# Layer 0's head norms take raw squares, and key weights are cast ahead of them

## The chip, the cores and the metric

The kernel runs on one core of a Trainium2 chip. The metric is the device time of one execution in microseconds, the median of several runs. A core has a matrix engine (TensorE, PE in the profile; its weight loads are PEld), a vector engine (VectorE, DVE), a scalar engine (ScalarE, ACT), GpSimd (POOL) and SyncE (SP), whose queue issues nearly all transfers. Each engine works through a queue of its own in a fixed order and waits on semaphores for the others.

## The reference

A two-layer encoder on 256 tokens of width 1024 (float32). What matters here is the beginning of a layer:

```python
u = rms_norm(h, g_mix_pre)
(gq, gk, gv, gg, ra_f, ra_b, aq, ak, av, gate_a, gate_b) = jnp.split(u @ w_in, offsets, axis=-1)
...
q = apply_axial_rope(rms_norm(aq.reshape(b, s, ATTN_HEADS, HEAD_DIM), g_q_norm), cos, sin)
k = apply_axial_rope(rms_norm(ak.reshape(b, s, ATTN_KV_HEADS, HEAD_DIM), g_k_norm), cos, sin)
```

Here `rms_norm(x, g)` is `x * rsqrt(mean(x*x) + 1e-6) * g`. There are 8 query heads and 2 key/value heads of 128. `ra_f` and `ra_b` are 16 columns each, the low-rank inputs of the decay of a gated linear attention (GLA). After that come both attentions, gates, an output projection, a feed-forward block and a per-layer embedding.

## The kernel before, in words

**Precision.** Every operand of a product is split into a high part (ScalarE casts it) and a low part (VectorE subtracts the cast from the source); three matmuls make one product. `split` does this for any tile (its lines are 132 and 128 of the profile).

**Weights.** All weights come in an ordered stream of units of about 1 MB. A unit is loaded into one of two raw buffers (`raw`), then cast into `wh` and subtracted into `wl`, each in two pieces (four such pairs of buffers); only after the subtraction is the raw buffer free for the next load. In layer 0, units 0 to 3 are the rows of the weights of the decay ranks and the queries together (1056 columns), units 4 and 5 the two halves of the key/value weights, units 6 and 7 those of the GLA queries. `Stream.fill` puts the splits of further units in the program as earlier ones are done. `ws.pieces` hands out the pieces of units 0 to 2, whose splits the start writes out by hand.

**Tokens.** The 256 tokens are two halves of 128 (`hf` 0 and 1).

**Start of layer 0.** The input norm is not applied to the tokens before the projection. `start` transposes raw blocks of `h` by TensorE into PSUM (`turn`), ScalarE scales by the gain column and casts (`high`), VectorE makes the low part (`rest`); the matmuls begin on these. `rstd` computes meanwhile, on GpSimd, the factor `rs[hf]` of each token: the sum of two mean squares and epsilon, then the power -1/2. It is multiplied in wherever the projection's results are read. A chain `on(engine, ...)` fixes the order of these instructions on each engine by hand. `warm_up` issues matmuls without a result in between.

**Ranks and queries** (`0rq`). For each half, three accumulators of 288, 384 and 384 columns take the product with units 0 to 3. When one is complete, `put_q` reads it: `put_ranks` (first accumulator only) scales the ranks into a zeroed tile with two columns of ones, which TensorE transposes some steps later (L987); `head_ss` squares each head on ScalarE with the sum beside it (L960), scaling by `rs`; `inv_sqrt` turns the sums into factors on GpSimd: add epsilon (L457), power (L458), and for layer 0 times `rs` (L461); `rope` rotates on VectorE (L125 twice, L954 once). The head's factor is used only in the softmax.

**Keys and values** (`0kv`). 48 matmuls of 512 columns with units 4 and 5 into two accumulators, one for each half; `keys` does the norm and rotation. Then come the GLA queries and keys (`0gqk`), the values and so on, with steps of the attention and the GLA put between the matmuls at fixed counts (`tick`).

**What sets the order.** Instructions are written in a program order; a planner places them in the queues before the run, by priority. `tc.high_priority(n)` moves a block ahead by n; `put_q` of layer 0 has `EMPTY_FIRST` = 1600. `tc.issue_after(ins)` puts the instructions of a block behind `ins` in the queue of that engine, without a semaphore. PSUM has eight banks, each an `acc` or `aux` tile.

Of the kernel before, what the change touches and what calls it, by code (L numbers as in the profile page):

```python
# [10 lines left out]
F32 = mybir.dt.float32  # L11
# [3 lines left out]
ALU = mybir.AluOpType  # L15
AX = mybir.AxisListType

P = 128
# [40 lines left out]
def trunk_kernel(ctx: ExitStack, tc: tile.TileContext, a: dict, out: bass.AP):  # L59
# [67 lines left out]
    def vsub(out, in0, in1):  # L127
        nc.vector.tensor_tensor(out=out, in0=in0, in1=in1, op=ALU.subtract)  # L128

    def split(hi, lo, src):  # L130

        nc.scalar.copy(hi, src)  # L132
        vsub(lo, src, hi.bitcast(F32))


    h = cp.tile([P, 2, D], F32, tag="h", name="h")
# [111 lines left out]
    class Stream:  # L248
# [7 lines left out]

        def __init__(self, depth):
            self.depth, self.held, self.room, self.ready, self.open = depth, 0, 0, [], False
            self.loads, self.jobs, self.lend = [], [], False
            pairs = {}  # L260
            for item in plan:
                if callable(item):
                    x = Load(item)
                    self.loads.append(x)
                    self.jobs.append(lambda x=x: self.plain(x))
                else:
                    units, n = item
                    if n == 1:
                        b11, b12, b21, b22 = units
                        x, z = (Load(b, lambda tag=tag: self.lent(tag), tag == "wh") for b, tag in ((b11, "wh"), (b12, "wl")))  # L270
                        y, q = Load(b22, big), Load(b21)
                        pairs[id(units)] = x, y, z, q
                        self.loads += [x, y, z]
                    if n == 5:
                        self.loads.append(q)
                    self.jobs.append(lambda p=pairs[id(units)], n=n: self.step(n, *p))
# [69 lines left out]

        def fill(self):
            while self.open and self.held < self.depth and self.jobs:
                pieces = self.jobs.pop(0)()
                for piece in pieces or ():  # L350
                    split(*piece)
                if pieces:
                    self.load()

        def take(self):
            self.fill()
# [5 lines left out]
            self.fill()  # L362

    ws = Stream(4)


    def gain(v, t, n):
# [83 lines left out]

        return tc.issue_after(last_pow[0].ins) if last_pow[0] is not None else nullcontext()

    def inv_sqrt(t, n, mul, add, by=None):

        with in_turn():
            nc.gpsimd.tensor_scalar(out=t, in0=t, scalar1=mul, scalar2=add, op0=ALU.mult, op1=ALU.add)  # L457
        last_pow[0] = nc.gpsimd.tensor_tensor(out=t, in0=t, in1=neghalf[:, :n], op=ALU.pow)  # L458
        if by is not None:
            with in_turn():  # L460
                last_pow[0] = nc.gpsimd.tensor_scalar(out=t, in0=t, scalar1=by, scalar2=None, op0=ALU.mult)  # L461

    def split_by(hi, lo, src, r):

# [289 lines left out]
    warm_up(WARM[1], True)  # L754
    uT = Split()
    ss = [small(2, "ss") for _ in range(2)]
    rs, ropes_first = [small(1, "rs", 2) for _ in range(2)], []

    up_first = [mid()]
    on("pool", nc.gpsimd.memset, up_first[0][0:81, :], 0.0)  # L760
# [9 lines left out]
    def rstd(hf):  # L770
        on("pool", nc.gpsimd.tensor_scalar,
           out=rs[hf], in0=ss[hf][:, 0:1], scalar1=ss[hf][:, 1:2], scalar2=EPS, op0=ALU.add, op1=ALU.add)
        on("pool", nc.gpsimd.tensor_tensor, out=rs[hf], in0=rs[hf], in1=neghalf[:, 0:1], op=ALU.pow)
        last_pow[0] = line["pool"]

# [37 lines left out]
    def start():  # L813
        cut = lambda piece, c: [t[:, c] for t in piece]
        gains()
        turn(0, 0)
        turn(1, 0)
        turn(0, 1)
        turn(1, 1)
        turn(0, 2, 3)  # L820
        warm_up(WARM[2], True)
        high(0, 0)
        high(1, 0)
        for c in RQ:
            on("act", nc.scalar.copy, *(t[:, slice(*c)] for t in unit_a[::2]))
        rest(0, 0)
        rest(1, 0)
        low(*cut(unit_a, slice(0, 288)))
        high(0, 1)
        high(1, 1)  # L830
        low(*cut(unit_a, slice(288, 1056)))
        on("act", nc.scalar.copy, unit_b[0], unit_b[2])
        rest(0, 1)
        rest(1, 1)
        high(0, 2, 3)
        low(*unit_b)
        rest(0, 2, 3)
        ws.load()
        unit_c, unit_d = ws.pieces()
        yield 2  # L840
        turn(1, 2, 3)
        high(1, 2, 3)
        rest(1, 2, 3)
        yield 4
        split_here(*unit_c)
        split_here(*unit_d)
        ws.load()
        for hf in range(2):
            square(hf, 0)
        yield 2  # L850
        turn(0, 4, 5, 6, 7)
        for hf in range(2):
            square_here(hf, 1)
            rstd(hf)
        ropes_first.extend(rope_tables(0))
        high(0, 4, 5, 6, 7)
        rest(0, 4, 5, 6, 7)
        yield 1
        turn(1, 4, 5, 6, 7)
        high(1, 4, 5, 6, 7)  # L860
        rest(1, 4, 5, 6, 7)
        for piece in ws.pieces():
            split_here(*piece)
        ws.load()
        ws.open = True
        ws.fill()
# [59 lines left out]
    for l in range(DEPTH):  # L926

        part[0] = f"{l}rq"
        rows = [None, None] if l else rs
        after_start = tc.issue_after(line["dma"].ins) if l == 0 else nullcontext()  # L930
        if l == 0:
            ropes = ropes_first
# [20 lines left out]
            )  # L953
            nc.vector.tensor_tensor(out=hv(dst), in0=hv(dst), in1=hv(t2), op=ALU.add)  # L954

        def head_ss(src, n, junk, ss, hf):
            by = {} if rows[hf] is None else {"scale": rows[hf]}
            for i in range(n):
                s = slice(i * P, (i + 1) * P)
                nc.scalar.activation(junk[:, s], src[:, s], AF.Square, accum_out=ss[:, i : i + 1], **by)  # L960

        def put_ranks(o, hf):

            r = t512()[:, 0:192].rearrange("p (d r) -> p d r", d=2)
            nc.gpsimd.memset(r, 0.0)
            for c in (16, 80):
                nc.gpsimd.memset(r[:, :, c : c + 1], 1.0)
            src = o[:, 0:32].rearrange("p (d r) -> p d r", d=2)  # L970
            with tc.high_priority(EMPTY):
                if rows[hf] is None:
                    nc.vector.tensor_copy(r[:, :, 0:16].bitcast(F32R), src)
                    vsub(r[:, :, 32:48].bitcast(F32R), src, r[:, :, 0:16])
                else:
                    nc.vector.tensor_scalar(
                        out=r[:, :, 0:16].bitcast(F32R), in0=src, scalar1=rows[hf], scalar2=None, op0=ALU.mult
                    )
                    nc.vector.scalar_tensor_tensor(
                        out=r[:, :, 32:48].bitcast(F32R), in0=src, scalar=rows[hf], in1=r[:, :, 0:16],  # L980
                        op0=ALU.mult, op1=ALU.subtract,
                    )
                nc.vector.tensor_copy(r[:, :, 64:80], r[:, :, 0:16])
            yield W["r"]
            ps = aux()
            for d in range(2):
                nc.tensor.transpose(ps[0:81, d * P : (d + 1) * P], r[:, d, 0:81], ident)  # L987
            nc.vector.tensor_copy(
                raT[:, :, hf * P : (hf + 1) * P], ps[0:81, 0 : 2 * P].rearrange("p (d t) -> p d t", d=2)
            )  # L990
# [7 lines left out]
        def put_q(hf, b, o):  # L998
            qr, ss = qrs[hf], qss[hf]
            with tc.high_priority(EMPTY if l else EMPTY_FIRST):  # L1000
                if b == 0:
                    ranks.append(Task(put_ranks(o, hf), part[0]))
                c0, c1 = RQ[b]
                lo = 32 if b == 0 else 0
                n, hd = (c1 - c0 - lo) // P, max(c0 - 32, 0) // P
                src, dst = o[:, lo : c1 - c0], qr[:, hd * P : (hd + n) * P]

                head_ss(src, n, dst, ss[:, hd : hd + n], hf)
                inv_sqrt(ss[:, hd : hd + n], n, 1.0, P * EPS, rows[hf])
                rope(src, n, ropes[0], hf, dst)  # L1010

        def rq_step(o, hf, b, u):
            c0, c1 = RQ[b]
# [40 lines left out]
        def keys(o):  # L1054
            krs = []
            for hf in range(2):
                with tc.high_priority(EMPTY):
                    kr = t512()
                    ss = small(2, "kss")
                    head_ss(o[hf], 2, kr, ss, hf)  # L1060
                    inv_sqrt(ss, 2, 1.0 / P, EPS, rows[hf])
                    rope(o[hf], 2, ropes[1], hf, kr)
                    s = slice(hf * 256, (hf + 1) * 256)
                    split_by(avh[:, s], avl[:, s], o[hf][:, 256:512], rows[hf])
                    for i in range(2):
                        s = slice(i * P, (i + 1) * P)
                        nc.vector.tensor_scalar(
                            out=kr[:, s], in0=kr[:, s], scalar1=ss[:, i : i + 1], scalar2=None, op0=ALU.mult
                        )
                krs.append(kr)  # L1070
# [575 lines left out]
```

## Time and profile before

| | |
|---|---|
| median of 3 runs | 926.07 us (925.95 to 927.97) |
| profiled execution, its own time | 926.16 us |
| its span | 924.1 us |
| TensorE busy | 911.3 us, 99% |
| VectorE busy | 785.4 us, 85% |
| ScalarE busy | 580.7 us, 63% |
| GpSimd busy | 88.5 us, 10% |
| granted TensorE clock | 0.998 |

How to read the lines below: in a timeline, a row is start, duration, engine, line of the kernel, operation, output tile <- input tiles, size, and count of merged instructions; in brackets stands the idle time of that engine just before it and what ended it. A tile's name carries the part of the program that made it (`wh_start`, `acc_0kv`). In the list of waits, a row is engine and tile, the releaser, total us, number of times, longest us. In the rows of stages, each engine has its busy us and its number of instructions, then the granted clock, the share of the DMA engines that is busy, and GB/s.

### The profile page before, as it was taken

How to read it: one execution, taken by the hardware profiler on the slowest of the kernel's cores; microseconds unless marked ns; L12 is line 12 of the kernel's file. 1: busy time of each engine (PE TensorE's matmuls, PEld its weight loads, DVE VectorE, ACT ScalarE, POOL GpSimd, SP SyncE). 2: the span in 40 equal slices, each digit the busy share in tenths (PEclk: the TensorE clock that was granted, in tenths of full speed). 3: DMA queues.
4: the chain of work that ended last, by engine and by line, in shares of the span. 5: the costliest groups of instructions: out<-in, count | busy, mean ns of one | idle time of the engine just before them, and what ended most of it. 6: DMA issues, size and time to landing. Idle time of an engine off the chain costs nothing.

```text
span 924.1 us, 12442 instructions
## 1 busy us (share of the span) xinstructions
PE 911.3 (99%) x4676; PEld 776.6 (84%) x4676; DVE 785.4 (85%) x1006; ACT 580.7 (63%) x959; POOL 88.5 (10%) x157
## 2 busy tenths in 40 slices
PE   9899999999999999999999999999999999999996
PEld 8798888888888888888899988888888888888885
DVE  6799989987678997999779789898876799989984
ACT  6479677664466655566666687765644766565563
POOL 2710211310000000000114001110001000000000
PEclk9999999999999999999999999999999999999999
DMA  8363455566386564737576524454573856556361
GB/s 291 124 219 134 138 182 188 178 211 220 104 271 229 162 248 160 273 115 258 200 255 212 173 92 137 137 184 180 185 251 107 282 178 203 214 178 225 133 232 45
DMA packets 88679, 173.44 MB, mean 188 GB/s; under 512 B 3422, under 2 KB 26470, under 8 KB 88108
## 3 DMA queue, kind: packets, MB, share of 16 engines
q1 hardware_dynamic: 88460, 172.40, 54.9%
q8 instruction: 36, 0.59, 0.3%
q10 hardware_dynamic: 160, 0.27, 0.1%
q14 instruction: 23, 0.19, 0.1%
HBM read 169.50 MB, written 3.15 MB: 187 GB/s over the span
## 4 chain that ended last, share of the span: by engine, by line
PE 93%; DVE 2%; ACT 1%; issue 1%; POOL 1%; DMA 1%; POOLq 0%; DVEq 0%; ACTq 0%; SPq 0%
PE acc_0ffnin L120 12%; PE acc_1ffnin L120 11%; PE acc_1gate L120 7%; PE acc_0gate L120 7%; PE acc_0ffnin L104 7%; PE acc_1ffnin L104 6%; PE acc_1rq L120 3%; PE acc_0wout L120 2%; PE acc_1gqk L120 2%; PE acc_1ple L120 2%; PE acc_0ple L120 2%; PE acc_1gg L120 2%; PE acc_0gg L120 2%; PE acc_0v L120 2%; PE acc_0merge L120 2%; PE acc_1merge L120 2%
## 5 line engine op out<-in xcount | busy, mean ns | idle before, releaser
L104 PE MATMUL acc_0ffnin<-wh_0ffnin,big_0ffnin 128*128 128x512 f32 x176 | 57.0, 393 | 0.0
L104 PE MATMUL acc_1ffnin<-wh_1ffnin,big_1ffnin 128*128 128x512 f32 x176 | 56.8, 393 | 0.0
L132 ACT CAST wh_1ffnin<-raw_1ffnin 128x1024 fp32r<-128x1024 f32 x38 | 38.5, 1049 | 25.9 <-PE acc_1ffnin L120 7.1
L132 ACT CAST wh_0ffnin<-raw_0ffnin 128x1024 fp32r<-128x1024 f32 x38 | 38.1, 1048 | 26.1 <-DMA raw_0ffnin<-in_w_ffn_out_dram 8.8
L128 DVE TENSOR_TENSOR wl_0ffnin<-raw_0ffnin,wh_0ffnin 128x1024 fp32r<-128x1024 f32 x38 | 44.7, 1220 | 9.1 <-ACT wh_0ffnin L132 9.0
L128 DVE TENSOR_TENSOR wl_1ffnin<-raw_1ffnin,wh_1ffnin 128x1024 fp32r<-128x1024 f32 x38 | 44.9, 1220 | 7.9 <-ACT wh_1ffnin L132 7.8
L120 PE MATMUL acc_1ffnin<-wh_1ffnin,big_1wout 128*128 128x512 f32 x168 | 42.5, 393 | 0.0
L120 PE MATMUL acc_0ffnin<-wh_0ffnin,big_0wout 128*128 128x512 f32 x168 | 42.5, 393 | 0.0
L104 PEld LDWEIGHTS acc_0ffnin<-wh_0ffnin,big_0ffnin 128*128 128x128 f32 x176 | 33.0, 188 | 7.1 <-DVE big_0ffnin L128 0.5
L104 PEld LDWEIGHTS acc_1ffnin<-wh_1ffnin,big_1ffnin 128*128 128x128 f32 x176 | 33.1, 188 | 6.7
L128 DVE TENSOR_TENSOR wl_1ffnin<-lent_1ffnin,wh_1ffnin 128x1024 fp32r<-128x1024 f32 x30 | 35.8, 1217 | 1.7 <-ACT wh_1ffnin L132 1.7
L128 DVE TENSOR_TENSOR wl_0ffnin<-lent_0ffnin,wh_0ffnin 128x1024 fp32r<-128x1024 f32 x30 | 35.8, 1217 | 0.7 <-ACT wh_0ffnin L132 0.7
L120 PEld LDWEIGHTS acc_1ffnin<-wh_1ffnin,big_1wout 128*128 128x128 f32 x168 | 31.1, 188 | 6.2
L120 PEld LDWEIGHTS acc_0ffnin<-wh_0ffnin,big_0wout 128*128 128x128 f32 x168 | 31.1, 188 | 6.2
L132 ACT CAST wh_1ffnin<-lent_1ffnin 128x1024 fp32r<-128x1024 f32 x30 | 30.6, 1052 | 7.1 <-PE acc_1ffnin L104 3.9
L132 ACT CAST wh_0ffnin<-lent_0ffnin 128x1024 fp32r<-128x1024 f32 x30 | 30.7, 1052 | 6.4 <-PE acc_0ffnin L104 3.9
L104 PE MATMUL acc_0ffnin<-wl_0ffnin,big_0ffnin 128*128 128x512 f32 x88 | 34.3, 390 | 0.0
L104 PE MATMUL acc_1ffnin<-wl_1ffnin,big_1ffnin 128*128 128x512 f32 x88 | 34.3, 390 | 0.0
L128 DVE TENSOR_TENSOR wl_0gate<-raw_0gate,wh_0gate 128x1024 fp32r<-128x1024 f32 x20 | 23.9, 1233 | 5.3 <-ACT wh_0gate L132 5.2
L128 DVE TENSOR_TENSOR wl_1gate<-raw_1gate,wh_1gate 128x1024 fp32r<-128x1024 f32 x20 | 23.6, 1219 | 5.4 <-ACT wh_1gate L132 5.4
L132 ACT CAST wh_1gate<-raw_1gate 128x1024 fp32r<-128x1024 f32 x20 | 20.0, 1049 | 11.7 <-DMA raw_1gate<-in_w_o_attn_dram 5.6
L132 ACT CAST wh_0gate<-raw_0gate 128x1024 fp32r<-128x1024 f32 x20 | 20.0, 1048 | 11.4 <-DMA raw_0gate<-in_w_o_attn_dram 5.6
(701 smaller groups left out, 2697.0 us busy)
## 6 DMA issues: line engine op xcount, KB each, us to landing
raw_0ffnin<-in_w_ffn_out_dram SPq DMA_DIRECT2D x11, 1024.0 KB, 5.6
raw_1ffnin<-in_w_ffn_out_dram SPq DMA_DIRECT2D x11, 1024.0 KB, 5.5
lent_0ffnin<-in_w_ffn_in_dram SPq DMA_DIRECT2D x6, 1024.0 KB, 7.5
lent_1ffnin<-in_w_ffn_in_dram SPq DMA_DIRECT2D x6, 1024.0 KB, 6.5
raw_0v<-in_w_in_dram SPq DMA_DIRECT2D x4, 1024.0 KB, 5.1
raw_0gate<-in_w_o_gla_dram SPq DMA_DIRECT2D x4, 1024.0 KB, 5.1
raw_0gate<-in_w_o_attn_dram SPq DMA_DIRECT2D x4, 1024.0 KB, 5.4
raw_0wout<-in_w_ffn_in_dram SPq DMA_DIRECT2D x8, 512.0 KB, 5.3
```

The source lines that it names most:

```text
L104: return nc.tensor.matmul(o, lhsT, rhs, start=start, stop=stop)
L120: nc.tensor.matmul(o, x, y, start=start and n == 0, stop=stop and n == len(seq) - 1, **kw)
L128: nc.vector.tensor_tensor(out=out, in0=in0, in1=in1, op=ALU.subtract)
L132: nc.scalar.copy(hi, src)
```

## The change

- **Epsilon.** For layer 0, the head squares are taken of the unscaled results. GpSimd makes in `rstd` a second value from the sum before the power, `he[hf]` = 128 * 1e-6 * (mean square of the token + 1e-6), and `inv_sqrt` adds it in place of the constant; the third step (L461) is dropped. With r the token's factor, r * (r²s + c)^-1/2 is (s + c/r²)^-1/2, and 1/r² is that sum. One instruction for each half enters between the sum and the power.
- **Rank constants.** In layer 0 VectorE, not GpSimd, writes the zeros and ones of the rank tile.
- **Casts and squares.** In `put_q` of layer 0, the head squares of half 0 stand in ScalarE's queue behind the cast of the last piece of unit 4, those of half 1 behind unit 5's; the rotations stand behind the matching subtractions in VectorE's queue. `split` returns both instructions for this, and the stream keeps them by the number of the unit.
- **Start.** ScalarE's first two `high` casts come after two transposes (block 0 of both halves), the three warm-up matmuls after these two transposes as well, and the other four transposes after the warm-ups. Before, all six transposes came first.

```diff
 def split(hi, lo, src):
-        nc.scalar.copy(hi, src)
-        vsub(lo, src, hi.bitcast(F32))
+        return nc.scalar.copy(hi, src), nc.vector.tensor_tensor(out=lo, in0=src, in1=hi.bitcast(F32), op=ALU.subtract)
...
         def fill(self):
             while self.open and self.held < self.depth and self.jobs:
+                n = self.total - len(self.jobs)
                 pieces = self.jobs.pop(0)()
                 for piece in pieces or ():
-                    split(*piece)
+                    self.last[n] = split(*piece)
...
+        def behind(self, n, which):
+            return tc.issue_after(self.last[n][which].ins)
...
-    def inv_sqrt(t, n, mul, add, by=None):
+    def inv_sqrt(t, n, mul, add, eps=None):
         with in_turn():
-            nc.gpsimd.tensor_scalar(out=t, in0=t, scalar1=mul, scalar2=add, op0=ALU.mult, op1=ALU.add)
+            if eps is None:
+                nc.gpsimd.tensor_scalar(out=t, in0=t, scalar1=mul, scalar2=add, op0=ALU.mult, op1=ALU.add)
+            else:
+                nc.gpsimd.tensor_scalar(out=t, in0=t, scalar1=eps, scalar2=mul, op0=ALU.add, op1=ALU.mult)
         last_pow[0] = nc.gpsimd.tensor_tensor(out=t, in0=t, in1=neghalf[:, :n], op=ALU.pow)
-        if by is not None:
-            with in_turn():
-                last_pow[0] = nc.gpsimd.tensor_scalar(out=t, in0=t, scalar1=by, scalar2=None, op0=ALU.mult)
...
     def rstd(hf):
         on("pool", nc.gpsimd.tensor_scalar,
            out=rs[hf], in0=ss[hf][:, 0:1], scalar1=ss[hf][:, 1:2], scalar2=EPS, op0=ALU.add, op1=ALU.add)
+        on("pool", nc.gpsimd.tensor_scalar, out=he[hf], in0=rs[hf], scalar1=P * EPS, scalar2=None, op0=ALU.mult)
...
         gains()
-        turn(0, 0)
-        turn(1, 0)
+        for hf in range(2):
+            turn(hf, 0)
+        for hf in range(2):
+            high(hf, 0)
+        warm_up(WARM[2], True)
         turn(0, 1)
         turn(1, 1)
         turn(0, 2, 3)
-        warm_up(WARM[2], True)
-        high(0, 0)
-        high(1, 0)
...
-        rows = [None, None] if l else rs
+        rows, eps = ([None, None], [None, None]) if l else (rs, he)
...
-                nc.scalar.activation(junk[:, s], src[:, s], AF.Square, accum_out=ss[:, i : i + 1], **by)
+                nc.scalar.activation(junk[:, s], src[:, s], AF.Square, accum_out=ss[:, i : i + 1])
...
-            nc.gpsimd.memset(r, 0.0)
+            fill = nc.gpsimd if l else nc.vector
+            fill.memset(r, 0.0)
             for c in (16, 80):
-                nc.gpsimd.memset(r[:, :, c : c + 1], 1.0)
+                fill.memset(r[:, :, c : c + 1], 1.0)
...
-                head_ss(src, n, dst, ss[:, hd : hd + n], hf)
-                inv_sqrt(ss[:, hd : hd + n], n, 1.0, P * EPS, rows[hf])
-                rope(src, n, ropes[0], hf, dst)
+                with ws.behind(4 + hf, 0) if l == 0 else nullcontext():
+                    head_ss(src, n, dst, ss[:, hd : hd + n])
+                inv_sqrt(ss[:, hd : hd + n], n, 1.0, P * EPS, eps[hf])
+                with ws.behind(4 + hf, 1) if l == 0 else nullcontext():
+                    rope(src, n, ropes[0], hf, dst)
...
-                    inv_sqrt(ss, 2, 1.0 / P, EPS, rows[hf])
+                    inv_sqrt(ss, 2, 1.0 / P, EPS, eps[hf])
```

More of the change, by code (lines that the diff above doesn't have):

```diff
@@ L258, in __init__ @@
             self.depth, self.held, self.room, self.ready, self.open = depth, 0, 0, [], False
-            self.loads, self.jobs, self.lend = [], [], False
+            self.loads, self.jobs, self.lend, self.last = [], [], False, {}
             pairs = {}
@@ L364, in trunk_kernel @@
     ws = Stream(4)
+    ws.total = len(ws.jobs)
     def gain(v, t, n):
@@ L756, in trunk_kernel @@
     ss = [small(2, "ss") for _ in range(2)]
-    rs, ropes_first = [small(1, "rs", 2) for _ in range(2)], []
+    rs, he = ([small(1, tag, 2) for _ in range(2)] for tag in ("rs", "he"))
+    ropes_first = []
     up_first = [mid()]
@@ L954, in rope, with head_ss @@
             nc.vector.tensor_tensor(out=hv(dst), in0=hv(dst), in1=hv(t2), op=ALU.add)
-        def head_ss(src, n, junk, ss, hf):
-            by = {} if rows[hf] is None else {"scale": rows[hf]}
+        def head_ss(src, n, junk, ss):
             for i in range(n):
                 s = slice(i * P, (i + 1) * P)
-                nc.scalar.activation(junk[:, s], src[:, s], AF.Square, accum_out=ss[:, i : i + 1], **by)
+                nc.scalar.activation(junk[:, s], src[:, s], AF.Square, accum_out=ss[:, i : i + 1])
         def put_ranks(o, hf):
             r = t512()[:, 0:192].rearrange("p (d r) -> p d r", d=2)
-            nc.gpsimd.memset(r, 0.0)
+            fill = nc.gpsimd if l else nc.vector
+            fill.memset(r, 0.0)
             for c in (16, 80):
-                nc.gpsimd.memset(r[:, :, c : c + 1], 1.0)
+                fill.memset(r[:, :, c : c + 1], 1.0)
             src = o[:, 0:32].rearrange("p (d r) -> p d r", d=2)
@@ L1059, in keys @@
                     ss = small(2, "kss")
-                    head_ss(o[hf], 2, kr, ss, hf)
-                    inv_sqrt(ss, 2, 1.0 / P, EPS, rows[hf])
+                    head_ss(o[hf], 2, kr, ss)
+                    inv_sqrt(ss, 2, 1.0 / P, EPS, eps[hf])
                     rope(o[hf], 2, ropes[1], hf, kr)
```

## The prediction

> **What bounds the kernel now.** I read the page first (busy shares, the chain that ended last), then the stages, then the waits of TensorE alone, and then the timeline of each engine around the one place that the waits named.
>
> ```profile
> span 924.1 us, 12442 instructions
> PE 911.3 (99%) x4676; PEld 776.6 (84%) x4676; DVE 785.4 (85%) x1006; ACT 580.7 (63%) x959; POOL 88.5 (10%) x157
> ...
> PE 93%; DVE 2%; ACT 1%; issue 1%; POOL 1%; DMA 1%; POOLq 0%; DVEq 0%; ACTq 0%; SPq 0%
> ...
> 200.00:900.00 700.00, 699.55 (x3483) 592.45 (x3482) 597.73 (x707) 435.82 (x676) 38.37 (x73) 1.00 0.57 194
> ```
>
> TensorE is the bound: 93% of the chain is its work, and in the 700 us of the row of stages (the first busy figure is PE's) it is idle for 0.45 us. Time can only come from where TensorE stands still. Its waits, all 924 us of them:
>
> ```profile
> PE acc_0kv L120 <- ACT wh_start L132: 1.2, 1, 1.2
> PE aux_0rq L987 <- DVE t_0rq L983: 1.1, 1, 1.1
> PE acc_0kv L120 <- DVE wl_start L128: 1.1, 2, 0.6
> ...
> PE acc_0rq L104 <- ACT wh_start L142: 0.4, 1, 0.4
> ...
> PEld acc_0gqk L120 <- DVE wl_0rq L128: 0.3, 1, 0.3
> ```
>
> The first three rows are one place, the key/value projection of layer 0 (acc_0kv), with the transposes of the decay ranks (L987) inside it. On TensorE's timeline:
>
> ```profile
> 31.88 2.14 PE L120 MATMUL acc_0kv<-wh_start,big_start 128*128 128x512 f32 x8
> 35.14 0.42 PE L987 MATMUL aux_0rq<-ident,t_0rq 128*81 128x128 f32 x2 [1.12 <-DVE t_0rq L983]
> 36.73 2.14 PE L120 MATMUL acc_0kv<-wh_start,big_start 128*128 128x512 f32 x8 [1.18 <-ACT wh_start L132]
> 44.91 1.98 PE L120 MATMUL acc_0kv<-wh_0rq,big_start 128*128 128x512 f32 x8
> 46.72 1.07 PE L120 MATMUL acc_0kv<-wl_0rq,big_start 128*128 128x512 f32 x4
> 47.63 0.61 PE L104 MATMUL aux_0kv<-mid_0kv 128*128 128x128 f32 x4
> ```
>
> Undisturbed, twelve of these matmuls start within 47.63 - 44.91 = 2.72 us. The projection has 48: 10.9 us, and 0.2 us for the two transposes. It takes 47.63 - 31.88 = 15.75 us, so 4.65 us are lost (the waits say 3.4; a busy time includes the drain of the last matmul, so I trust the starts). Why the weights are late stands in ScalarE's queue:
>
> ```profile
> 27.99 0.37 ACT L960 ACTIVATE mid_0rq<-acc_0rq,rs_start 128x128 f32<-128x128 f32 x1 [5.24 <-DVE t_0rq L983]
> 30.74 1.08 ACT L132 CAST wh_start<-raw_start 128x1024 fp32r<-128x1024 f32 x1
> 34.94 0.37 ACT L960 ACTIVATE mid_0rq<-acc_0rq,rs_start 128x128 f32<-128x128 f32 x1 [1.01 <-DVE t_0rq L979]
> 35.64 1.04 ACT L132 CAST wh_start<-raw_start 128x1024 fp32r<-128x1024 f32 x1
> 36.57 2.01 ACT L132 CAST wh_0rq<-raw_start 128x1024 fp32r<-128x1024 f32 x2
> ```
>
> ScalarE idles 5.24 us before the first head square at 27.99. Eight squares follow, then half of unit 4 (the first key/value unit) is cast at 30.74, the squares of half 1 come next, and the second half is cast only at 35.64, unit 5 behind it. Were the weights there earlier?
>
> ```profile
> 24.00:25.00 1.00, 1.00 (x7) 1.00 (x6) 0.85 (x1) 0.00 (x0) 1.00 (x2) 1.00 0.22 82
> 29.00:30.00 1.00, 1.00 (x9) 1.00 (x8) 0.97 (x3) 1.00 (x8) 0.82 (x3) 1.00 0.23 86
> 24.87 16.57 SPq L297 DMA_DIRECT2D raw_start<-in_w_in_dram  x2
> SPq L297 <- DVE wl_start L128: 19.9, 2, 15.7
> ```
>
> The DMA traffic of unit 4 dies down between 24 and 25 us (last two columns: share and GB/s), and unit 5, issued at 24.87, between 29 and 30. So unit 4 lay in SBUF some 6 us before its cast, unit 5 some 7. The next load then waits 15.7 us for the subtraction that frees unit 4's raw buffer.
>
> **The change, part by part.**
>
> ```profile
> 27.34 0.25 DVE L976 TENSOR_SCALAR t_0rq<-acc_0rq,rs_start 128x32 fp32r<-128x32 f32 x1 [2.49 <-PE acc_0rq L120]
> 34.03 0.25 DVE L976 TENSOR_SCALAR t_0rq<-acc_0rq,rs_start 128x32 fp32r<-128x32 f32 x1 [1.59 <-POOL t_0rq L967]
> 34.90 1.34 DVE L125 TENSOR_TENSOR mid_0rq<-acc_0rq,rope_start 128x384 f32<-128x384 f32 x3
> 40.97 2.35 DVE L128 TENSOR_TENSOR wl_0rq<-raw_start,wh_0rq 128x1024 fp32r<-128x1024 f32 x2
> 16.74 0.57 POOL L142 TENSOR_TENSOR rs_start<-rs_start,neghalf 128x1 f32<-128x1 f32 x1
> 33.48 0.31 POOL L461 TENSOR_SCALAR qss_0rq<-qss_0rq,rs_start 128x3 f32<-128x3 f32 x1
> 33.73 0.26 POOL L967 MEMSET t_0rq<- 128x192 f32 x1
> 40.26 2.02 POOL L461 TENSOR_SCALAR qss_0rq<-qss_0rq,rs_start 128x3 f32<-128x3 f32 x1
> ```
>
> *Casts ahead of squares.* Unit 4's two casts (2.0 us by the 36.57 row) run at about 24.9 to 26.9, where ScalarE idled; its subtractions (2.35 us) at 26 to 28.4 on VectorE, half of it in the 2.49 us that stood idle. The squares of half 0 start at 28 to 28.5, eight in 2.75 us (27.99 to 30.74), end by 31.2; unit 5 is cast 31.2 to 33.2, then the squares of half 1, to 36. TensorE reaches unit 4 at 31.88 with both its parts complete, unit 5 at 31.88 + 5.44 + 0.2 = 37.5 with its cast over since 33.2. The four starved places of the projection go: -4.65.
>
> *Rank constants.* The memset of half 1 now queues on GpSimd behind the powers of half 0 (33.48, 33.73), and L976 waits 1.59 us for it. On VectorE it waits for none of that. This removes the 35.14 wait, already in the 4.65; both edits are needed for it. Six memsets come to VectorE. Nearest rows: 0.26 on GpSimd for 128x192, and as lower bound nothing, where they fall into idle time. I take 0.5 us of VectorE for those that do not, off TensorE's path.
>
> *Epsilon.* Eight third steps (L461; 0.31 to 2.02 us each, the long ones beside VectorE's subtractions) leave GpSimd, and two multiplications enter between the sum and the power of rs. Each costs 0.31 to 2.02 by the same rows, nearest to the short one, for nothing heavy runs beside it: rs is ready by 16.74 + 0.57 + 2 x 0.4 = 18, at the worst 21.4, and first read at 27.34. Cost zero. The head norms' results are read by the softmax, much later; gain zero too.
>
> *What is late next.* VectorE. From 26 on it owes, until the query/key projection needs unit 6: subtractions of units 4, 5 and 6 (7.05), two ropes of three times three operations at up to 0.45 (2 x 3.9), ranks, memsets, rank and diagonal copies (about 2.5, an estimate of ten operations at the 0.25 of the 27.34 row): 17.4 us, plus about 1 waiting for the first squares, ends at 44.4. TensorE, no longer starved, reaches unit 6 at 31.88 + 11.1 + 0.4 = 43.4 and its low part 1 us later. The loads are no limit: unit 6's load is released at 28.4 instead of about 41 (24.87 + 16.57 less the issue itself). So VectorE is just in time. I keep 0.5 us lost (0 to 1.5 as bounds), and take the 0.3 us of the gqk row as gone, its weights being earlier.
>
> *Start.* Two transposes, their casts, the warm-ups, then four transposes.
>
> ```profile
> 4.56 1.20 PE L142 MATMUL aux_start<-ident,h 128*128 128x128 f32 x6
> 5.60 0.81 PE L104 MATMUL warm<-keep,seed 128*128 128x512 bf16 x3
> 5.80 0.62 ACT L142 ACTIVATE big_start<-aux_start,gcol_start 128x128 fp32r<-128x128 f32 x2 [2.68 <-PE aux_start L142]
> 6.20 0.61 DVE L142 SCALAR_TENSOR_TENSOR big_start<-aux_start,gcol_start,big_start 128x128 fp32r<-128x128 f32 x2 [1.37 <-ACT big_start L142]
> 6.80 2.40 PE L104 MATMUL acc_0rq<-wh_start,big_start 128*128 128x288 f32 x12 [0.39 <-ACT wh_start L142]
> 11.72 2.43 DVE L142 TENSOR_TENSOR wl_start<-raw_start,wh_start 128x1056 fp32r<-128x1056 f32 x2 [0.33 <-ACT wh_start L142]
> 14.10 0.51 PE L120 MATMUL acc_0rq<-wl_start,big_start 128*128 128x288 f32 x2
> ```
>
> Six transposes start 0.17 us apart. With only two ahead, ScalarE could begin at about 5.0 instead of 5.80, and TensorE at 6.4 instead of 6.80: -0.39, its wait. Two rows cap that. At 14.10 TensorE takes the low part whose subtractions end at 14.15; it is just in time there, so an earlier start is spent waiting, save about 0.1. And the squares at 27.99 and 34.94 wait for L979/L983, though both only read the accumulator: accesses of two engines to one PSUM tile are kept apart in program order. VectorE's first subtraction at 6.20 reads the bank into which the late transposes now write ahead of it, and so moves to about 6.6, against the gain. The Trainium skill says the same in "PSUM — Partial Sum Buffer", section "PSUM bank collisions raise a hardware error": the hardware does not arbitrate two engines in one bank, so software must order them. The two waits agree; without this rule the start would be worth up to 0.39 until 14.10. I take 0, bounds -0.4 to +0.4.
>
> **The sum.** -4.65 - 0.3 + 0.5 + 0 = -4.45. The profiled execution took 926.16 (2.1 more than its span), the median of three runs is 926.07: 921.6 to 921.7. TensorE is never starved for long after 50 us, so what is won at 43 stays won.
>
> **The rivals.**
> (a) *The gap closes in part.* The order in each queue is made before the run, from priorities. If half 1's rank operations stand on VectorE behind both subtractions of unit 5 (33.2 + 2.35 = 35.6, then 0.5), the transposes that TensorE met in the old run after eight key matmuls, at 33.7, wait until some 36.1: 2.4 us of the 4.65 stay. If the subtractions of unit 4 stand behind the first rope, one or two of the other places stay, near 1.2 each by the waits. 923 to 924.5. For it: VectorE's load above. Against: the ranks have the higher priority in the code, and their input is complete at about 30.
> (b) *Nothing to measure.* If the loads were the limit, the casts could not move: the DMA rows speak against it. Or VectorE's 17.4 us stretch until TensorE waits at unit 6 for all it won: the low part would come at 44.4 + 4.95 = 49.4, so VectorE would have to idle for 5 us more than I have. 925 to 927.
> (c) *Slower: weights push ahead of the attention on VectorE.*
>
> ```profile
> 50.00:100.00 50.00, 49.96 (x341) 46.28 (x342) 47.07 (x82) 39.26 (x76) 2.11 (x4) 1.00 0.51 169
> ```
>
> After the projections VectorE is busy for 47.07 of 50 us, while it serves the weights, the softmax and the gated attention at once. Units that come earlier can be queued ahead of softmax or decay operations whose results TensorE meets at a fixed place of its own queue. Each such swap puts two subtractions, 2.35 us, in front of a step; one that has no slack costs 2.35. Two swaps cost 4.7 and eat the gain; from three on it is slower, 7.05 - 4.95 = +2.1, with four +4.45: 928.2 to 930.5. For it: 2.9 us of idle VectorE in 50 are little. Against it: TensorE is busy for 49.96 of these 50 us, so the steps now have slack, and priorities there are unchanged.
>
> **How the numbers follow.** Forecast 0.69 (920.6 to 923), (a) 0.12, (b) 0.09, (c) 0.10. A measurement here can tell 0.2%, 1.9 us, from no change, so the bounds are 924.2 and 927.9: faster is the forecast and most of (a), 0.78; same the rest of (a) and (b), 0.12; slower (c), 0.10. The range 920.4 to 925.0 takes in the forecast with the bounds of the start and of VectorE, and (a); above it lie (c) and most of (b).
>
> **What would show it.** In the changed profile the waits on acc_0kv and on L987 should be gone from TensorE's list, the projection should last about 11.1 us, the first key cast should start near 25 with the idle 5.24 us cut, the load released at about 41 should go out before 31, and L461 be absent. If acc_0kv starts at 31.9 and ends after 45, the queue orders of (a) are the reason; if it ends at 43 and the time is still 925 or more, the loss is at unit 6 (b) or in the attention (c); a first matmul much after 6.8 would be the start.

## The result, and the profile after

The changed kernel takes 933.79 us (median; 932.52 to 934.97), the kernel before 926.52 in the same comparison: a ratio of 1.0077 [1.0064, 1.0090], 7.3 us slower. The forecast was 921.7, the range 920.4 to 925.0. The prediction is wrong by 12 us and in its sign, though the gap that it set out to close did close. The profiled execution of the changed kernel took 932.52, its span 930.7, 6.6 more than before. From its page, the span and the busy shares:

```profile
span 930.7 us, 12440 instructions
PE 911.6 (98%) x4676; PEld 777.3 (84%) x4676; DVE 787.6 (85%) x1012; ACT 578.8 (62%) x959; POOL 83.8 (9%) x145
```

TensorE's busy time has not moved (911.6 against 911.3), so the 6.6 us are time in which it stands still. TensorE's waits, in full:

```profile
PE aux_0kv L104 <- DVE mid_0kv L882: 9.7, 1, 9.7
PE warm L104 <- POOL seed L141: 1.0, 1, 1.0
PE aux_1at L104 <- DVE mid_1at L132: 0.2, 1, 0.2
```

All the waits that the prediction named are gone. One new one, of 9.7 us, has come. TensorE's timeline around it, and ScalarE's and SyncE's rows that belong to the prediction's steps:

```profile
31.43 2.07 PE L120 MATMUL acc_0kv<-wh_start,big_start 128*128 128x512 f32 x8
36.74 0.38 PE L993 MATMUL aux_0rq<-ident,t_0rq 128*81 128x128 f32 x2
41.77 1.07 PE L120 MATMUL acc_0kv<-wl_0rq,big_start 128*128 128x512 f32 x4
52.57 1.20 PE L104 MATMUL aux_0kv<-mid_0kv 128*128 128x128 f32 x4 [9.73 <-DVE mid_0kv L882]
...
25.15 2.00 ACT L132 CAST wh_start<-raw_start 128x1024 fp32r<-128x1024 f32 x2 [2.52 <-DMA raw_start<-in_w_in_dram]
29.82 2.00 ACT L132 CAST wh_0rq<-raw_start 128x1024 fp32r<-128x1024 f32 x2
48.49 1.99 ACT L132 CAST wh_0kv<-raw_0rq 128x1024 fp32r<-128x1024 f32 x2 [2.87 <-DMA raw_0rq<-in_w_in_dram]
...
30.01 0.37 SPq L296 DMA_DIRECT2D raw_start<-in_w_in_dram  x1
```

Unit 4 is cast at 25.15, unit 5 at 29.82, the next load goes out at 30.01, and the projection runs from 31.43 without a pause; four matmuls from 41.77 at the pace of 2.72 us for twelve end it at 42.68. Then TensorE stands still until 52.57. What it waits for, `aux_0kv <- mid_0kv`, is a small product: `spread_rows` multiplies a matrix of ones by a diagonal matrix of the tokens' factors `rs`, so that the factors lie along the columns. VectorE makes the diagonal from the identity, once for each half, 0.47 us for both (`nc.vector.tensor_scalar`, L876 before, L882 after). `rs` itself is ready at 17.9 us. The first two rows below are VectorE's of the kernel before, the others of the changed kernel:

```profile
43.90 0.47 DVE L876 TENSOR_SCALAR mid_0kv<-ident,rs_start 128x128 f32<-128x128 f32 x2
...
47.63 2.36 DVE L128 TENSOR_TENSOR wl_0rq<-raw_start,wh_0rq 128x1024 fp32r<-128x1024 f32 x2
```

```profile
41.89 1.21 DVE L132 TENSOR_TENSOR wl_0rq<-raw_start,wh_0rq 128x1024 fp32r<-128x1024 f32 x1
43.03 0.74 DVE L125 TENSOR_TENSOR t_0kv<-acc_0kv,rope_start 128x256 f32<-128x256 f32 x2
...
44.36 0.76 DVE L125 TENSOR_TENSOR t_0kv<-acc_0kv,rope_start 128x256 f32<-128x256 f32 x2 [0.27 <-ACT t_0kv L965]
45.04 0.75 DVE L960 TENSOR_TENSOR t_0kv<-t_0kv,t_0kv 128x256 f32<-128x256 f32 x2
45.70 0.87 DVE L472 SCALAR_TENSOR_TENSOR big_0kv<-acc_0kv,rs_start,big_0kv 128x256 fp32r<-128x256 f32 x2
46.49 0.86 DVE L1075 TENSOR_SCALAR t_0kv<-t_0kv,kss_0kv 128x128 f32<-128x128 f32 x4
47.27 2.35 DVE L132 TENSOR_TENSOR wl_0rq<-raw_0rq,wh_0rq 128x1024 fp32r<-128x1024 f32 x2
...
49.88 2.35 DVE L132 TENSOR_TENSOR wl_0kv<-raw_0rq,wh_0kv 128x1024 fp32r<-128x1024 f32 x2
52.15 0.47 DVE L882 TENSOR_SCALAR mid_0kv<-ident,rs_start 128x128 f32<-128x128 f32 x2
```

Before, the diagonal stood ahead of unit 6's subtractions (47.63) and was ready 3.3 us ahead of its use. In the changed kernel the planner put it behind the subtractions of units 6, 7 and 8, and behind the rotation, the norm and the low parts of the keys and values (43.03 to 47.27). By the starts of the rows, TensorE's 9.7 us are 4.5 for the subtractions of units 7 and 8, 3.6 for the key and value operations, 0.7 for two copies of the ranks, and 0.6 for the end of unit 6 and the diagonal itself. VectorE stands still for only 0.27 us of them: the load that ScalarE waits for at 48.49 doesn't hold it up. Nothing that the diagonal reads is late; its place in VectorE's queue is.

The idle time has a price of its own. TensorE's stages of 1 us (busy us and instructions, granted clock, DMA share, GB/s):

```profile
44.00:45.00 1.00, 0.00 (x0) 1.00 0.70 88
45.00:46.00 1.00, 0.00 (x0) 0.72 1.02 342
46.00:47.00 1.00, 0.00 (x0) 0.50 1.03 399
...
55.00:56.00 1.00, 1.00 (x8) 0.66 1.05 408
56.00:57.00 1.00, 1.00 (x10) 1.00 0.74 279
```

A row between two rates tells by its mean where the step lies: the clock falls to half at 45.44, 2.6 us into the idle time, and rises at 55.68, 3.1 us after the work began. The Trainium skill ("TensorE: Matmul & The Clock Gate", Part 1, on the clock gate) has half rate after an idle window and full rate after a busy one, the window of 3.41 us running freely. The trace agrees: fall and rise lie 10.24 us apart, three such windows. What the low clock costs is read from the stretch between the spread product and the first value matmul: 47.63 to 77.20 before, 29.6; 52.57 to 83.13 after, 30.6. About 1 us.

The tally of the span: -4.95 at the end of the projection (42.68 for 47.63), +9.89 until the spread product starts, +1.0 for the clock, +0.1 on the way to layer 1, and +0.5 in its first projection, where TensorE has gaps for which the trace names no releaser. Together they make the 6.6. Two of the experiments below (the chain with the early diagonal, the late diagonal) lose 0.3 us at that place and the others nothing; the 0.5 stays unexplained.

### The profile page after: what moved, and what is told of

It reads as the page before. It is cut to its first block, busy times and chain, and to the rows that moved or that the text cites. A ratio compares the mean times of both kernels' runs of the same rounds, so it can differ in the third digit from the quotient of the medians.

```text
span 930.7 us, 12440 instructions
## 1 busy us (share of the span) xinstructions
PE 911.6 (98%) x4676; PEld 777.3 (84%) x4676; DVE 787.6 (85%) x1012; ACT 578.8 (62%) x959; POOL 83.8 (9%) x145
## 4 chain that ended last, share of the span: by engine, by line
PE 87%; DVE 4%; DMA 3%; ACT 2%; issue 2%; POOL 1%; SPq 0%; POOLq 0%; DVEq 0%; ACTq 0%
PE acc_0ffnin L120 12%; PE acc_1ffnin L120 11%; PE acc_1gate L120 7%; PE acc_0gate L120 7%; PE acc_0ffnin L104 6%; PE acc_1ffnin L104 6%; PE acc_0gqk L120 3%; PE acc_0wout L120 2%; PE acc_1gqk L120 2%; PE acc_1ple L120 2%; PE acc_1gg L120 2%; PE acc_0gg L120 2%; PE acc_0v L120 2%; PE acc_0merge L120 2%; PE acc_1merge L120 2%; PE acc_1rq L120 2%
## 5 line engine op out<-in xcount | busy, mean ns | idle before, releaser
L132 ACT CAST wh_0gate<-raw_0gate 128x1024 fp32r<-128x1024 f32 x20 | 20.0, 1050 | 11.3 <-DMA raw_0gate<-in_w_o_attn_dram 5.4
```

Of the source, the lines that this page charges most:

```text
L132: return nc.scalar.copy(hi, src), nc.vector.tensor_tensor(out=lo, in0=src, in1=hi.bitcast(F32), op=ALU.subtract)
```

## The experiments

The theory is that the change closes the gap, and that the diagonal's place in VectorE's queue loses more than that: move the diagonal alone, and the forecast comes true. Its main rival is that VectorE simply has too much to do by then, so that the wait would move to unit 6 or to the attention. Every ratio is to runs of the kernel before on the same chip.

**The diagonal early.** The changed kernel, and in `spread_rows`:

```diff
-            nc.vector.tensor_scalar(out=diag[:, s], in0=ident, scalar1=rs[hf], scalar2=None, op0=ALU.mult)
+            with tc.high_priority(EMPTY_FIRST):
+                nc.vector.tensor_scalar(out=diag[:, s], in0=ident, scalar1=rs[hf], scalar2=None, op0=ALU.mult)
```

> The changed kernel with one edit: the two products that make the diagonal of the tokens' factors (L882) are given the priority of the query work, so that they leave their place behind the subtractions of unit 8 in VectorE's queue. Theory A (one misplaced VectorE step is the whole loss): the 9.7 us wait of TensorE at aux_0kv goes, the clock stays at 1.00 after it, the key/value phase still ends near 42.7; about 10.9 us faster than the changed kernel, 921.5 to 923. Rival B (VectorE and the loads are the bound, the diagonal only shows it): TensorE waits instead at the low parts of units 7 and 8, whose subtractions ended at 49.5 and 52.2, by 3 us or more; 925 or above.

Measured: 921.08 us (920.47 to 922.21) against 926.26, ratio 0.9943 [0.9931, 0.9955], a little better than the theory had it. Its timeline, and its stages (busy us of PE, PEld, DVE, ACT, POOL, then clock, DMA share, GB/s):

```profile
35.64 0.48 DVE L883 TENSOR_SCALAR mid_0kv<-ident,rs_start 128x128 f32<-128x128 f32 x2
42.82 0.60 PE L104 MATMUL aux_0kv<-mid_0kv 128*128 128x128 f32 x4
```

```profile
24.00:43.00 19.00, 19.00 (x101) 17.01 (x100) 16.67 (x36) 10.75 (x42) 13.98 (x23) 1.00 0.51 172
43.00:56.00 13.00, 13.00 (x112) 13.00 (x112) 11.03 (x24) 7.25 (x15) 1.84 (x3) 1.00 0.50 170
```

The diagonal comes at 35.64, TensorE is busy for all of the 32 us from 24 to 56, and the span is 920.4. The priority of this one line (two instructions) is worth 12.4 us by the two ratios. The rival falls: VectorE has the same work, and the wait does not move elsewhere. This is the fastest version of those measured here, 5.2 us faster than before.

**Without the chain.** The changed kernel, with both `ws.behind(...)` contexts around `head_ss` and `rope` replaced by `nullcontext()`.

> The changed kernel without the order of squares and rotations behind the casts and subtractions; epsilon, VectorE's rank constants and the start stay. Theory A: the order is what displaced the diagonal; without it the diagonal stands ahead of unit 6's subtractions again, no wait at aux_0kv, some of the old waits at acc_0kv come back: 923.5 to 927. Rival C (VectorE's memsets or the start displaced it): 932 or above, with the wait at aux_0kv.

Measured: 925.42 (923.73 to 928.15), ratio 0.9985 [0.9975, 0.9995]. TensorE's wait at the projection, the diagonal, and two stages of TensorE:

```profile
PE acc_0kv L120 <- DVE wl_start L132: 2.1, 1, 2.1
```

```profile
42.29 0.47 DVE L882 TENSOR_SCALAR mid_0kv<-ident,rs_start 128x128 f32<-128x128 f32 x2
```

```profile
38.00:39.00 1.00, 0.00 (x0) 0.98 0.00 0
42.00:43.00 1.00, 1.00 (x5) 0.82 1.06 408
```

The waiting is half there again (2.1 us of 3.4), and the diagonal is back at 42.29, ahead of its use at 47.06. The chain is both the gain and the loss. The pause of 2.1 us lets the clock fall too, from about 38.96 to 42.36. So the projection still lasts 15.50 us (31.56 to 47.06) for the 15.75 of before, and the spread product starts only 0.6 us earlier, although 1.3 us less of waiting is listed.

**The chain alone.** The kernel before with `split`'s return value, `Stream.last`, `Stream.behind` and the two contexts; epsilon, rank constants and start as before.

> The kernel before with the order behind casts and subtractions alone; epsilon, rank constants and start as before. Theory A: the diagonal stands behind unit 8's subtractions, TensorE waits for it at aux_0kv until some 52 us whatever happened earlier; 932 to 935. Rival C: no such wait, 921 to 926.

Measured: 935.27 (934.7 to 936.48), ratio 1.0097 [1.0084, 1.0110], at the upper end of what the theory expected.

```profile
PE aux_0kv L104 <- DVE mid_0kv L880: 10.9, 1, 10.9
```

```profile
35.51 0.25 DVE L980 TENSOR_SCALAR t_0rq<-acc_0rq,rs_start 128x32 fp32r<-128x32 f32 x1 [1.58 <-POOL t_0rq L971]
```

The same wait, 10.9 us long, from the chain alone. The second row bears on the rank constants: VectorE waits 1.58 us for GpSimd's memset as in the kernel before, but TensorE does not wait for the ranks. The planner has moved their transposes too; in this run they stand behind 21 key matmuls, in the changed kernel behind 23 (the row at 36.74), in the kernel before behind 8.

**The chain and the early diagonal.** The kernel of the last experiment, with the edit of the first.

> The kernel before with the order of squares and rotations behind the casts, and the diagonal early; epsilon, rank constants and start as before. With the order alone the key/value projection ended at 43.2 instead of 42.7 and had no wait in it, although L976's operation still waited 1.58 us for GpSimd's memset. Theory A: the order and the diagonal's place carry the gain, the other edits some 0.5 us: 921.5 to 922.8. The prediction's step that VectorE's rank constants are needed as well: 1.4 us or more of the gain lost, 923 to 924.5.

Measured: 922.74 (921.82 to 922.96), ratio 0.9951 [0.9938, 0.9963].

```profile
36.51 0.38 PE L992 MATMUL aux_0rq<-ident,t_0rq 128*81 128x128 f32 x2
```

The transposes at 36.51 wait for nothing (a wait would stand in brackets), although VectorE waits 1.58 us for the memset here too. Two edits, the chain and the diagonal's priority, give 4.5 of the 5.3 us; what epsilon, rank constants and start add to them, 0.7 by the two ratios, lies within the intervals, which overlap.

**The diagonal late, nothing else.** The kernel before, with the stream's infrastructure, and the diagonal put behind the subtractions of unit 8:

```diff
+            with ws.behind(8, 1):
                 nc.vector.tensor_scalar(out=diag[:, s], in0=ident, scalar1=rs[hf], scalar2=None, op0=ALU.mult)
```

> The kernel before with one edit: the two products of the diagonal are put behind unit 8's subtractions in VectorE's queue (which ended at 58.6 there), where the changed kernel has them; squares, casts, epsilon, constants and start as before. Theory A: TensorE waits at aux_0kv from 47.6 until about 58.8, 11 us, the clock falls after it (1 us): 937 to 939. Rival B (the place of the diagonal only shows a bound of VectorE and the loads): under 930.

Measured: 939.63 (939.14 to 942.46), ratio 1.0142 [1.0123, 1.0162], 0.6 us above the range of the theory and far from the rival's.

```profile
PE aux_0kv L104 <- DVE mid_0kv L881: 11.0, 1, 11.0
```

```profile
58.54 0.48 DVE L881 TENSOR_SCALAR mid_0kv<-ident,rs_start 128x128 f32<-128x128 f32 x2
```

The bad place alone, in a kernel that has none of the change's other parts, makes the same wait. The profile's span is 13.8 us longer: 11.3 at the start of the spread product (58.97 for 47.63), 2.1 in the stretch to the first value matmul (58.97 to 90.65, 31.7 for 29.6), and 0.3 in the first projection of layer 1. The stretch costs 1.1 more than in the changed kernel, and the stages say why:

```profile
51.00:52.00 1.00, 0.00 (x0) 0.50 0.54 113
63.00:64.00 1.00, 1.00 (x6) 0.50 0.02 6
64.00:65.00 1.00, 1.00 (x8) 0.67 0.04 8
```

The clock stays at half until 64.66, 5.7 us after the work began, where the changed kernel had 3.1. From its fall at 51.0 that is 13.66 us, four windows of 3.41. The work began 1.1 us into the third of them (57.83 to 61.24), and the 2.3 us that were left of it did not bring the clock back; in the changed kernel it began 0.3 us into a window (52.27 to 55.68), and 3.1 us did. What an idle time costs behind its end so depends on where it ends in the window.

**The clock.** The changed kernel, with matmuls without a result put on TensorE between the projection and the spread product, 36 of them in one run and 44 in the other:

```diff
+        idle = aux()
+        for _ in range(36):
+            with tc.issue_after(last_mm[0].ins):
+                last_mm[0] = nc.tensor.matmul(idle, seed, keep, start=True, stop=True)
```

> The changed kernel with 36 matmuls without a use (bf16, 512 columns, about 8 us) put into TensorE's queue between the key/value projection and the wait at aux_0kv. Theory D (the granted clock fell to 0.54 after the wait, and that cost about 1 us): the clock stays at 1.00 and the time falls by 0.8 to 1.2 us against the changed kernel. Rival E (the extra us after the wait has another cause): no change, or slower by what the useless matmuls delay.

> As the run with 36 useless matmuls, but with 44, which at 0.227 us each reach to 52.7, where the diagonal comes. With 36 the array still stood idle for 2 us and the clock fell to 0.50 all the same, from 53.9 to 57.3. Theory D: with no idle time left the clock stays at 1.00 and the stretch from the diagonal's matmuls to the value projection is as long as in the kernel before (29.6 us, against 30.5 in the changed one); about 1 us faster than the changed kernel. Rival E: the stretch stays at 30.5.

Measured with 36: 932.18 (930.65 to 934.63), ratio 1.0061 [1.0049, 1.0073]; with 44: 932.80 (932.44 to 933.51), ratio 1.0066 [1.0054, 1.0079]. With 36, the useless work ends at 50.67; TensorE's timeline and stages:

```profile
52.72 0.68 PE L104 MATMUL aux_0kv<-mid_0kv 128*128 128x128 f32 x4 [2.05 <-DVE mid_0kv L888]
```

```profile
53.00:54.00 1.00, 1.00 (x10) 0.93 1.09 424
54.00:55.00 1.00, 1.00 (x6) 0.50 1.00 383
57.00:58.00 1.00, 1.00 (x9) 0.86 0.00 0
```

Here the expectation failed: 2.05 us of idle time were enough for the clock to fall. It fell at 53.86, 1.1 us after the work had begun again, and rose at 57.28, one window later. The stretch to the values is 30.6 us (52.72 to 83.36), no better than in the changed kernel. So the time, 1.5 us below the changed kernel's by the ratios (with overlapping intervals), where 0.8 to 1.2 was expected, is not the clock's doing. With 44:

```profile
53.55 0.68 PE L104 MATMUL aux_0kv<-mid_0kv 128*128 128x128 f32 x4 [1.25 <-DVE mid_0kv L888]
```

```profile
56.00:57.00 1.00, 1.00 (x11) 1.00 1.05 408
```

The pause of 1.25 us left the clock alone, and the stretch is 29.2 us (53.55 to 82.70). The diagonal came 1 us later in this run, and in layer 1 TensorE waits 1.0 us at a place where the changed kernel doesn't, so the profile's span shows nothing of it. The clock's part is seen in the stretches: 30.6 us where it fell and rose behind the wait, 29.6 in the kernel before, 29.2 here, and 29.0 with the diagonal early (42.82 to 71.81), so 1.0 to 1.6 us. The times alone, 0.1% apart, don't tell it.

**The small parts, each alone in the kernel before.** Rank constants on VectorE:

> The kernel before with VectorE writing the constants of the rank tile, alone. Theory A: the 1.59 us wait of L976 for GpSimd goes and with it the wait of the rank transposes, but the casts of units 4 and 5 are still late, so TensorE waits for these instead; 0 to 1 us faster. Rival G (the wait for the ranks is worth its own 1.4 us): 1.2 us faster or more.

Start (two transposes, two casts, warm-ups, four transposes):

> The kernel before with the new order of the start alone. From the changed kernel's trace, where the rank transposes began at 31.30 instead of 31.54: theory A says 0.2 to 0.3 us faster, 925.9 to 926.2. Rival F (the subtraction that moved behind the late transposes holds the start up, as the prediction's bound of +0.4 had it): 0 to 0.4 slower.

Epsilon (`he` in place of the third step, squares without the factor):

> The kernel before with epsilon carrying the mean square, alone. The squares lose their scale operand and took 0.25 us a head instead of 0.34 in the changed kernel's trace, so ScalarE casts unit 4 by up to 16 x 0.09 = 1.4 us earlier: theory A says 0.5 to 1.4 us faster. The prediction's price was nothing: within 0.3 us of the kernel before.

Measured: ranks 924.40 (923.97 to 926.11), ratio 0.9978 [0.9969, 0.9987]; start 927.06 (925.68 to 927.80), 1.0001 [0.9992, 1.0009]; epsilon 925.78 (924.78 to 928.62), 0.9995 [0.9986, 1.0004]. TensorE's waits at the projection with the ranks alone, then with epsilon alone:

```profile
PE acc_0kv L120 <- DVE wl_start L128: 1.3, 1, 1.3
PE acc_0kv L120 <- ACT wh_start L132: 0.7, 1, 0.7
```

```profile
PE acc_0kv L120 <- DVE wl_start L128: 2.4, 2, 2.0
```

The memset's move removes the wait at the rank transposes by itself and starts the spread product at 45.48 instead of 47.63: 2.0 us faster, where the theory had at most 1; the rival, that the wait is worth its own length, was right. Once the chain is there, that wait is gone without it. The times of start and epsilon can't be told from no change, but epsilon's profile does show an effect: unit 5's casts start at 34.35 instead of 36.57, and the spread product at 46.50 instead of 47.63.

## Why the prediction was wrong, point by point

**The gap: right, in mechanism and nearly in size.** The projection lasts 11.25 us (31.43 to 42.68), 11.1 was said; that is 4.50 less than the 15.75 of before, for the 4.65 forecast. Its end comes 4.95 earlier, and that this is just -4.65 - 0.3 is luck: the rest is 0.45 by which the projection starts earlier, while the 0.3 stood for another wait, at unit 6. The first cast, the load, the vanished waits came as foretold.

**VectorE's time for unit 6: right.** Unit 6's low part was reckoned to end at 44.4; the row at 41.89 ends at 43.1, with copies and the diagonal, which were in the sum, left for later. In the first experiment, with the diagonal ahead of it, the same row ends 0.2 us later, and TensorE doesn't wait at unit 6.

**The step that failed is "what is late next".** It summed what VectorE owes and asked when the sum ends, with the diagonal as one of ten small operations in "about 2.5". A sum by duration holds only if the order within it stays. The diagonal's duration is 0.47 us; its place cost 9.7, because the planner wrote a new order in which the subtractions of two further units (4.5 us) and the key and value operations (3.6 us), none of them in the sum, stand ahead of it. The conclusion "what is won at 43 stays won" was drawn from 850 us in which TensorE had no gap in the old order, which is no evidence on the new. Why the planner's priorities come out so was not tried; that the chain alone makes it do so was.

**The rivals.** (c) had the right kind of mechanism, units that come earlier standing on VectorE ahead of a step which TensorE meets at a fixed place, and it got 0.10. Its place was wrong (the spread product at 43, not the softmax or decay from 50 on), its price too: counted as 2.35 for each pair of subtractions, where the wait also holds 3.6 us of key and value operations, and 1 us of clock comes on top. Its sign was right. (a) is refuted by the changed kernel itself, where nothing of the gap stays, (b) by the first experiment, where VectorE is in time.

**"Both edits are needed" for the rank wait: wrong.** Either is enough, the memset on VectorE (alone 2.0 us) or the chain (alone, it puts the transposes 13 matmuls later). A place on TensorE that was taken as fixed had moved as well.

**Start at 0: right,** as far as it can be told: its interval, -0.7 to +0.8 us, holds 0 and -0.39 alike, and in the profile of that run the rank transposes come at 31.34 instead of 31.54. The rule of the Trainium skill ("PSUM — Partial Sum Buffer", section "PSUM bank collisions raise a hardware error"), by which the start was put at 0 rather than -0.39, has software keep two engines out of one bank. The trace shows such an order kept: VectorE's first subtraction starts at 7.00 instead of 6.20, behind TensorE's four late transposes. What the chip would do without it no run shows. And the low part that TensorE took at 14.10 is taken at 14.01, the 0.1 us that the prediction left over.

**Epsilon at 0: not settled.** Its interval is -1.3 to +0.4 us, and the reason given for no gain, that the norms' results are read late, left out that ScalarE's squares get shorter (0.25 us apart for 0.34) and the key casts earlier with them.

## What to carry to other kernels

When a change makes inputs come earlier under a planner, go through every step that the bounding engine meets at a fixed place, the cheap ones first, and ask for each what may now be queued ahead of it: a step has a place in a queue as well as a duration, and only the duration is in the old profile. A small operation whose inputs have long been ready and whose result is needed soon should carry a priority of its own; here that turned +7.3 us into -5.2. And an idle time of TensorE costs more than its length where the clock falls with it.

## What the runs showed of the hardware

Every step of the granted clock in these traces lies a whole number of windows of 3.41 us from the one before: 10.24 us in the changed kernel, 13.66 with the diagonal late, 3.42 and 3.40 after the pauses of 2.05 and 2.11 us. So a window need not be idle in full for the clock to fall, as the "idle window" of the Trainium skill ("TensorE: Matmul & The Clock Gate", Part 1) might be read: the 2.05 us, 60% of the window that ended at 53.86, were enough. A pause of 1.25 us left it at 1.00, and so did one of 1.98 us in the run with epsilon alone. Whether that one was too short or lay across the end of a window isn't settled.

Nor need it be one pause. In the run with the start alone, TensorE has two pauses at the places of the kernel before, 1.15 and 1.18 us:

```profile
34.95 0.42 PE L987 MATMUL aux_0rq<-ident,t_0rq 128*81 128x128 f32 x2 [1.15 <-DVE t_0rq L983]
36.55 3.49 PE L120 MATMUL acc_0kv<-wh_start,big_start 128*128 128x512 f32 x8 [1.18 <-ACT wh_start L132]
```

Its granted clock is 0.50 from 36.90 to 40.32, and the eight matmuls, 2.14 us in the kernel before, take 3.49. Both pauses lie in the 3.41 us that end at 36.90. The run with the diagonal late shows the same (0.50 from 37.34 to 40.76), while in the profile of the kernel before two such pauses, 1.12 and 1.18 us, left the clock at 1.00. So short pauses can add up, but they don't always. A pause of two microseconds can thus cost a third one, and a long one can cost what is left of a window and one more at half rate behind its end.

A head square on ScalarE is cheaper without a factor for each partition. In the changed kernel, and with epsilon alone, the squares start 0.25 us apart, in the kernel before 0.34 (0.36 to 0.44 us each there):

```profile
27.73 0.28 ACT L965 ACTIVATE mid_0rq<-acc_0rq 128x128 f32<-128x128 f32 x1 [0.58 <-DVE t_0rq L989]
```
